# A two-layer hybrid encoder on one core: every TensorE operand moved to a multiple of 512 bytes in SBUF

## The chip, the core and the metric

The kernel runs on one core of one Trainium2 chip. It has five engines that run their own instruction streams and meet at semaphores: TensorE (PE in the profile; PEld is its loading of the stationary operand), VectorE (DVE), ScalarE (ACT), GpSimd (POOL) and SyncE (SP), which issues most of the DMAs. Operands lie in SBUF, a memory of 128 partitions; a tile has an address, which is the byte inside a partition at which it begins. TensorE reads two operands from SBUF for a matmul, the stationary one (128x128 here) and the moving one (128 rows by up to 512 columns), and writes to PSUM. The metric is the device time of one execution in microseconds (us); a time is the median over several runs.

## What is computed

The input is one sequence of 512 positions with 1024 features, in float32. There are two layers, each with a mixer and an MLP, and a last norm:

```python
for layer in range(DEPTH):                      # DEPTH = 2
    h = rms_norm(x, norm_mix[layer])
    y = stick_breaking_attention(h, ...) if layer == 0 else rglru_block(h, ...)
    x = x + y
    h = rms_norm(x, norm_mlp[layer])
    u = relu(h @ w1[layer])                     # 1024 -> 4096
    x = x + (u * u) @ w2[layer]                 # 4096 -> 1024
return rms_norm(x, norm_final)
```

The attention has 16 heads of 64. It takes sigmoids of the scores, a cumulative product of what each key leaves over (from right to left), and sums the values with the weights that result. The second mixer projects to 2048 features, runs a causal convolution with four taps, two gates of block-diagonal 64x64 matrices, and a linear recurrence over the positions (a scan), and multiplies by a gelu branch before its output projection.

## The kernel before

**Precision by halves.** TensorE is fed in a type (float32r) that keeps fewer bits than float32. So each operand is split into a high part (a rounded copy, made by ACT) and a low part (what is left, made by DVE's subtraction), and each product is three matmuls: high by high, low by high and high by low. `three` (L217 to L221) does that for a weight as the stationary operand and 512 positions as the moving one. xgh and xgl hold the halves of the layer's normed input, bh and bl those of the next product's input; these four tiles of 16 KB per partition lie in the pool `const`. Weights come by DMA in slabs of 128 partitions by 1024 numbers (`raw`), and their halves are wh and wl, four of each in the pool `wpool`.

**The MLPs.** Each MLP is cut in four quarters of 1024 hidden features. Most of its products are done by a scheme of seven block products in place of eight (`PRODUCTS`, P1 to P7), whose operands are sums of blocks. In the up products (L966) the weight is stationary and the moving operand has 256 columns: parts of xgh and xgl, or the sums s41 with the low parts `low`, or parts of bh and bl. In the down products (L1061) the hidden features are stationary (bh and bl for the first half, sh and sl for the second) and the weight moves with 512 columns. Helper lines stand for many operations: L757 is the one line in which the class `Ordered` records all of an MLP's DVE and ACT work, so it has to be read by tiles.

**The order.** The order on TensorE is written out by the program. In the attention the products of the next heads are filled in between the scores and values of the current ones by due times (`PACE`, `SCORE0`, `VAL0`); in the second mixer the string `ORDER` gives it; in the MLPs `run` steps through the products and prepares operands up to five products ahead. The other engines' instructions are ordered by a planner, except where the code ties one behind another (`issue_after`, `Ordered`).

**Where tiles lie.** A pool is a stretch of SBUF; pools are laid one behind the other, and a pool that closes gives its place to the next one. Inside a pool the tiles stand in the order in which their tags are first used, `bufs` copies of each, and every tile is rounded up to 32 bytes. The first pool starts at byte 1152. Before the change `const` holds colt (384 bytes), ones and ident (512 each), eps (4), then xgh, xgl, bh, bl, and at its end eight tiles `lams` of 32 bytes. Then follow `wpool` (three raw, four wh, four wl, of 4096 bytes each), `work` (ssq, two sq and two r of 2048 bytes, then the small rt, rc, rp, rn and rr), `home` (eight tiles of 2048 bytes) and the pools of a stage: `hp` and `sp` in the attention, `wmore`, `rp1` and `rp2` in the second mixer, `mlp0` or `mlp1` with `blocks0` or `blocks1` in the MLPs. In `sp` the four `last` tiles (1024 bytes) stand behind three scan tiles of 513 numbers. Ahead of the second MLP's pool a small pool `last` holds three tiles of 4, 48 and 16 bytes.

Of the kernel before, what the change touches and what calls it, by code (L numbers as in the profile page):

```python
# [11 lines left out]
F32 = mybir.dt.float32  # L12
F32R = mybir.dt.float32r
AF = mybir.ActivationFunctionType
ALU = mybir.AluOpType
PSUM = bass.MemoryType.PSUM

P = 128
S = 512
D = 1024  # L20
C = D // P
# [3 lines left out]
EPS = 1e-6  # L25
RG_C = 8.0
SCALE = HD ** -0.5


START = [  # L30
# [31 lines left out]
def hybrid_encoder(  # L62
# [24 lines left out]
    V, A, G, PE = nc.vector, nc.scalar, nc.gpsimd, nc.tensor  # L87

    const = ctx.enter_context(tc.tile_pool(name="const", bufs=1))
    wpool = ctx.enter_context(tc.tile_pool(name="wpool", bufs=4))  # L90
    work = ctx.enter_context(tc.tile_pool(name="work", bufs=2))
# [11 lines left out]
    def f(ap):  # L103
        return ap.bitcast(F32)
# [11 lines left out]
    make_identity(nc, ident)  # L116
    eps_t = const.tile([P, 1], F32, tag="eps", name="eps_t")
    V.memset(eps_t, EPS)

    xgh = const.tile([P, C, S], F32R, tag="xgh", name="xgh")  # L120
    xgl = const.tile([P, C, S], F32R, tag="xgl", name="xgl")
# [19 lines left out]
    class Squares:  # L141
# [21 lines left out]
        def inv_squares(self, ps):  # L163

            for t in range(S // P):
                PE.matmul(
                    ps[:, t : t + 1], self.acc[:, t * P : (t + 1) * P], ones[:, 0:1],
                    start=True, stop=True,
                )
            n = S // P  # L170
            rr = work.tile([P, 2 * n], F32, tag="rr", name="rr", bufs=1)
            V.tensor_scalar(rr[:, :n], ps[:, :n], 1.0 / D, EPS, ALU.mult, ALU.add)
            V.reciprocal(rr[:, :n], rr[:, :n])
            V.tensor_scalar(rr[:, n:], rr[:, :n], -1.0, None, ALU.mult)
            return rr


# [53 lines left out]
    def beside(ws, ah, al, pss, at, ks=range(C)):  # L231
# [8 lines left out]
    ctx.enter_context(tc.manual_schedule(engines={mybir.EngineType.PE}))  # L240


    lams = {
        n: const.tile([P, C], F32, tag=f"lam_{n}", name=n)
        for n in ("ab", "pp", "den", "s1", "s2", "pl", "c8", "c4")
    }
    c8, c4 = lams["c8"], lams["c4"]

    def softplus():

        ab, pp, den, s1, s2, pl, _, _ = lams.values()
        lam = col("lam")

        sigmoid = yield
        V.tensor_scalar(ab, lam, -1.0, None, ALU.mult)
        V.tensor_tensor(ab, ab, lam, ALU.max)
        with tc.issue_after(sigmoid.ins):
            A.activation(pp, ab, AF.Sigmoid, scale=-1.0)
        with tc.issue_after((yield).ins):
            V.tensor_scalar(den, pp, -1.0, 2.0, ALU.mult, ALU.add)  # L260
        V.reciprocal(den, den)
        V.tensor_tensor(s1, pp, den, ALU.mult)
        V.tensor_tensor(s2, s1, s1, ALU.mult)
        V.tensor_scalar(pl, s2, 1.0 / 17, 1.0 / 15, ALU.mult, ALU.add)
        for n in (13, 11, 9, 7, 5, 3, 1):
            V.tensor_tensor(pl, pl, s2, ALU.mult)
            V.tensor_scalar(pl, pl, 1.0 / n, None, ALU.add)
        V.tensor_tensor(pl, pl, s1, ALU.mult)
        V.tensor_scalar(den, lam, -1.0, 0.0, ALU.mult, ALU.max)
        V.scalar_tensor_tensor(c8, pl, 2.0, den, ALU.mult, ALU.add)  # L270
        V.tensor_scalar(c4, c8, RG_C * 0.5, None, ALU.mult)
        V.tensor_scalar(c8, c8, -RG_C, None, ALU.mult)
        yield
# [5 lines left out]
    NB = S // P  # L279
    PAIRS = H // 2  # L280
    half = [slice(0, HD), slice(HD, P)]
    so, early = {}, {}
# [4 lines left out]
    def home_tile(tag, n, name):  # L287
        return home.tile([P, S], F32, tag=tag, name=name, bufs=n)

    with ExitStack() as actx:  # L290
        hp = actx.enter_context(tc.tile_pool(name="hp", bufs=2))
        sp = actx.enter_context(tc.tile_pool(name="sp", bufs=1))


        later = sp.tile([P, S], F32, tag="later", name="later")
        G.memset(later, 0.0)
        G.affine_select(
# [11 lines left out]
        for i in range(2):  # L309
            both = []  # L310
            for nm in ("h", "l"):
                t = sp.tile([P, 2 * P], F32R, tag=f"last{nm}{i}", name=f"last{nm}{i}")
                G.memset(f(t[:, :P]), 0.0)
                both.append(t)
            lasts.append(both)
# [117 lines left out]
        def inverse():  # L433
# [9 lines left out]
            with tc.high_priority():  # L443
                norm["root"] = A.activation(rc, pc[:, :NB], AF.Sqrt, bias=eps_t, scale=1.0 / D)
                V.reciprocal(rc, rc)
                for t in range(NB):
                    ts = slice(t * P, (t + 1) * P)
                    V.tensor_scalar(diag[:, ts], ident, rc[:, t : t + 1], None, ALU.mult)
                V.tensor_scalar(rp, rc, SCALE, None, ALU.mult)
                V.tensor_scalar(rn, rc, -SCALE, None, ALU.mult)  # L450
            norm.update(rc=rc, rp=rp, rn=rn)
# [861 lines left out]
    with ExitStack() as mctx:  # L1313
        mlp = Mlp(mctx, 0)
# [4 lines left out]
        last = {}  # L1319
# [22 lines left out]
        def between(c):  # L1342
            nc.sync.dma_start(out=away[:, c, :], in_=x[c])
            if c == C - 1:
                soft.send(mlp.ready)
# [235 lines left out]


    with ExitStack() as mctx:
        lp = mctx.enter_context(tc.tile_pool(name="last", bufs=1))
        mlp = Mlp(mctx, 1)

        def between(c):

            t = c - 1
            if t not in range(NB):  # L1590
                return
            for h in range(2):
                pt = mlp.bank()
                for i in range(4):
                    PE.transpose(
                        pt[:, i * P : (i + 1) * P], x[4 * h + i][:, t * P : (t + 1) * P], ident
                    )
                A.copy(mlp.y(t, h), pt)
                mlp.begun.add((t // 2 * 2 + h, t % 2))

        gb = []

        def factors():
            for h in range(2):
                gb.append(home_tile(*HOMES[h], "gb"))
                nc.sync.dma_start(
                    out=gb[h], in_=g_final[:, h * S : (h + 1) * S].broadcast_to([P, S])
                )


        A.activation(lp.tile([P, 1], F32, tag="rt", name="early"), eps_t, AF.Sqrt)

        ss = lp.tile([P, NB, 3], F32, tag="ss", name="ss")
        bias = lp.tile([P, NB], F32, tag="bias", name="bias")

        def square(t, h, i, cols=slice(0, S), end=False):

            junk = work.tile([P, S], F32, tag="sq", name="junk")
            A.activation(
                junk[:, cols], mlp.y(t, h)[:, cols], AF.Square, accum_out=ss[:, t, i : i + 1]  # L1620
            )
            if not end:
                A.activation(
                    bias[:, t : t + 1], ss[:, t, i : i + 1], AF.Identity,
                    bias=bias[:, t : t + 1] if i else eps_t, scale=1.0 / D,
                )

        def scaled(t, h, cols=slice(0, S)):
            y = mlp.y(t, h)[:, cols]
            G.tensor_tensor(y, y, gb[h][:, cols], ALU.mult)  # L1630

        def finish(t, h, i, cut=None, last=None):

            ts = slice(t * P, (t + 1) * P)
            rt = work.tile([P, 1], F32, tag="rt", name="rt")
            A.activation(rt, ss[:, t, i : i + 1], AF.Sqrt, bias=bias[:, t : t + 1], scale=1.0 / D)
            V.reciprocal(rt, rt)
            done, y = mlp.y(t, 1 - h), mlp.y(t, h)
            A.activation(done, done, AF.Copy, scale=rt)
            nc.sync.dma_start(out=out[ts, (1 - h) * S : (2 - h) * S], in_=done)  # L1640
            with tc.issue_after(last.ins) if last else nullcontext():
                V.scalar_tensor_tensor(
                    y[:, cut:], y[:, cut:], rt, gb[h][:, cut:],
                    ALU.mult, ALU.mult,
                )
            if cut:
                V.tensor_scalar(y[:, :cut], y[:, :cut], rt, None, ALU.mult)
            nc.sync.dma_start(out=out[ts, h * S : (h + 1) * S], in_=y)

        def end(ws, xs):  # L1650
            for t in range(2):
                square(t, 0, 0)
                scaled(t, 0)
                square(t, 1, 1, end=True)
                finish(t, 1, 1, last=mlp.gained)
            for t in range(2, 4):
                square(t, 1, 0)
                scaled(t, 1)
            for g in range(2):
                mlp.times("P4", g, 0, ws[g], xs[0], False)  # L1660
            mlp.collect("P4", 0, xs[0])
            square(2, 0, 1, end=True)
            finish(2, 0, 1)
            mlp.collect("P4", 1, xs[1])
            for i in range(2):
                cols = slice(i * HS, (i + 1) * HS)
                ps = mlp.bank()[:, :HS]
                for g in range(2):
                    mlp.times("P4", g, 1, ws[g], ps, True, cols)
                mlp.collect("P4", 1, ps, cols)  # L1670
                square(3, 0, 1 + i, cols, end=i == 1)
                if i == 0:
                    scaled(3, 0, cols)
            finish(3, 0, 2, HS)

        end.ready = factors
        mlp.quarters(between, end)
# [69 lines left out]
```

## Time and profile before

| | |
|---|---|
| median of three runs | 1048.85 us (1048.2 to 1051.05) |
| the profiled execution, first to last instruction | span 1047.9 us; its own time is not listed apart from the three runs |
| TensorE busy | 1035.1 us (99%), 5868 matmuls |
| loading of stationary operands | 902.8 us (86%) |
| DVE, ACT, POOL busy | 863.1 us (82%), 701.5 us (67%), 179.2 us (17%) |
| moved by DMA | 159.41 MB, 152 GB/s on average |

Busy times come from one profiled execution. Matmuls overlap: each lasts longer than the distance to the next one's start, because a result needs time to come out of the array. So a matmul's mean duration is not its cost; the distance between the starts of neighbours is, and it is read from the timeline, or from the chain of waits, which merges a run of like matmuls into one row with its length and count ("5.47 PE ps_t L1061 x24"). In a row such as `ps_t<-wh,bh` the names are those of the output, of the moving operand and of the stationary one.

### The profile page before, as it was taken

What the parts mean: (1) busy time and instruction counts of PE and PEld (TensorE: products, weight loads), DVE (VectorE), ACT (ScalarE), POOL (GpSimd) and SP (SyncE); (2) the same over time, 40 slices, a digit from 0 to 9 for tenths busy, and PEclk for the clock granted to TensorE, in tenths of its full rate; (3) what the DMA queues carried; (4) which work ended last, traced back from release to release, by engine and by line L of the source; (5) the groups of instructions that cost most, each with busy time, mean ns of one, the idle gap of its engine ahead of it and who ended that gap; (6) DMA issues with size and microseconds to landing.
All of it is one profiled execution on the core that took longest, in us unless ns stands there. A gap on an engine that the chain in (4) does not pass through costs nothing.

```text
span 1047.9 us, 15859 instructions
## 1 busy us (share of the span) xinstructions
PE 1035.1 (99%) x5868; PEld 902.8 (86%) x5868; DVE 863.1 (82%) x1147; ACT 701.5 (67%) x1082; POOL 179.2 (17%) x238
## 2 busy tenths in 40 slices
PE   8999999999999999999999999999999999999997
PEld 7888888888888988988988788888888988988986
DVE  7888787848788898898899799984789797897897
ACT  6767676836766773773775699964755773773775
POOL 2344344420000010010011121200000010010013
PEclk9999999999999999999999999999999999999999
DMA  6745354537536667567582483352345667567553
GB/s 225 204 137 141 101 149 104 153 109 274 149 80 190 181 139 204 165 140 207 164 208 81 109 214 112 91 221 93 88 86 173 174 142 206 158 139 204 145 125 101
DMA packets 52828, 159.41 MB, mean 152 GB/s; under 512 B 6672, under 2 KB 7952, under 8 KB 52752
## 3 DMA queue, kind: packets, MB, share of 16 engines
q1 hardware_dynamic: 41808, 120.13, 34.4%
q0 software_dynamic: 10368, 37.75, 20.9%
q8 instruction: 46, 0.75, 0.3%
q10 hardware_dynamic: 576, 0.52, 0.2%
q14 instruction: 30, 0.25, 0.1%
HBM read 137.41 MB, written 4.19 MB: 135 GB/s over the span
## 4 chain that ended last, share of the span: by engine, by line
PE 88%; DVE 5%; ACT 3%; issue 2%; DMA 2%; ACTq 0%; POOL 0%; DVEq 0%; POOLq 0%
PE ps_t L1061 14%; PE ps_acc L966 8%; PE ps_z L966 8%; PE ps_acc L1061 7%; PE ps_acc L219 5%; PE ps_acc L221 5%; PE ps_acc L220 5%; PE ps_o L966 5%; PE ps_z L1061 4%; PE ps_o L219 2%; PE ps_t L220 2%; PE ps_o L220 2%; PE ps_o L221 2%; PE ps_t L221 2%; PE ps_t L219 2%
## 5 line engine op out<-in xcount | busy, mean ns | idle before, releaser
L757 ACT CAST wh<-b 128x1024 fp32r<-128x1024 f32 x168 | 174.0, 1047 | 125.6 <-DVE b L757 76.7
L757 DVE TENSOR_TENSOR wl<-b,wh 128x1024 fp32r<-128x1024 f32 x168 | 203.8, 1221 | 50.5 <-ACT wh L757 50.1
L1043 POOL DMA_DIRECT2D b<-in_w_dn x40 | 35.0, 875 | 360.9 <-DVE b L757 204.6
L219 PE MATMUL ps_acc<-xgh,wh 128*128 128x512 f32 x192 | 78.5, 409 | 0.0
L221 PE MATMUL ps_acc<-xgl,wh 128*128 128x512 f32 x192 | 75.2, 392 | 0.0
L220 PE MATMUL ps_acc<-xgh,wl 128*128 128x512 f32 x192 | 75.1, 391 | 0.0
L581 DVE TENSOR_TENSOR_SCAN scan<-keep,later 128x128 f32<-128x128 f32 (+1 forms) x64 | 59.6, 933 | 18.8 <-ACT keep L571 10.9
L214 DVE TENSOR_TENSOR wl<-raw,wh 128x512 fp32r<-128x512 f32 (+2 forms) x70 | 60.9, 895 | 16.2 <-ACT wh L212 16.1
L757 ACT ACTIVATE u<-u 128x512 f32<-128x512 f32 x100 | 63.1, 632 | 6.5 <-DVE u L757 4.8
L212 ACT CAST wh<-raw 128x512 fp32r<-128x512 f32 (+2 forms) x70 | 50.8, 759 | 23.1 <-PE ps_acc L221 7.3
L1043 POOL DMA_DIRECT2D b<-in_w_up x24 | 20.8, 867 | 240.5 <-DVE b L757 72.1
L585 POOL TENSOR_TENSOR w<-w,scan 128x128 f32<-128x128 f32 (+1 forms) x64 | 51.9, 813 | 55.9 <-DVE scan L581 53.2
L757 DVE TENSOR_TENSOR b<-b,b 128x1024 f32<-128x1024 f32 x48 | 58.7, 1224 | 1.3
L757 DVE TENSOR_TENSOR u<-u 128x512 f32<-128x512 f32 (+1 forms) x92 | 54.9, 596 | 2.7 <-ACT u L757 1.1
L966 PE MATMUL ps_z<-xgh,wh 128*128 128x256 f32 x192 | 54.2, 282 | 0.0
L966 PE MATMUL ps_z<-xgh,wl 128*128 128x256 f32 x192 | 54.1, 282 | 0.0
L757 ACT CAST wh<-raw 128x1024 fp32r<-128x1024 f32 x46 | 47.9, 1045 | 9.3 <-PE ps_acc L1061 8.4
L966 PE MATMUL ps_acc<-low,wh 128*128 128x256 f32 x192 | 53.6, 279 | 0.0
L1061 PE MATMUL ps_t<-wl,sh 128*128 128x512 f32 x126 | 50.1, 398 | 0.0
L1061 PE MATMUL ps_t<-wh,sh 128*128 128x512 f32 x126 | 49.6, 394 | 0.0
L1061 PE MATMUL ps_t<-wh,sl 128*128 128x512 f32 x126 | 49.4, 392 | 0.0
L1061 PE MATMUL ps_t<-wh,bh 128*128 128x512 f32 x126 | 49.2, 391 | 0.0
(399 smaller groups left out, 3434.4 us busy)
## 6 DMA issues: line engine op xcount, KB each, us to landing
b<-in_w_dn SPq DMA_DIRECT2D x48, 512.0 KB, 4.5
b<-in_w_dn POOLq DMA_DIRECT2D x40, 512.0 KB, 5.5
b<-in_w_up SPq DMA_DIRECT2D x36, 512.0 KB, 4.6
b<-in_w_up POOLq DMA_DIRECT2D x24, 512.0 KB, 5.3
raw<-in_w_m SPq DMA_DIRECT2D x16, 512.0 KB, 4.1
raw<-in_w_dn SPq DMA_DIRECT2D x16, 512.0 KB, 4.7
raw<-in_w_in SPq DMA_DIRECT2D x16, 512.0 KB, 4.2
raw<-in_w_qk SPq DMA_DIRECT2D x12, 512.0 KB, 3.7
```

Source lines behind the costliest of these rows:

```text
L212: A.copy(wh[:, k, :], raw[:, k, :])
L214: V.tensor_tensor(wl[:, k, :], raw[:, k, :], f(wh[:, k, :]), ALU.subtract)
L219: PE.matmul(ps, wh, ah, start=start, stop=False)
L220: PE.matmul(ps, wl, ah, start=False, stop=False)
L221: PE.matmul(ps, wh, al, start=False, stop=stop)
L581: V.tensor_tensor_scan(sc[:, S - n : S][:, ::-1], keep[:, :n][:, ::-1], later[:, S - n :][:, ::-1], 1.0, ALU.mult, ALU.max,)
L585: G.tensor_tensor(wt, wt, sc[:, S - n + 1 : S + 1], ALU.mult)
L757: ins = getattr(self.e, name)(*args, **kwargs)
L966: PE.matmul(ps[:, i * HS : (i + 1) * HS], m, y, start=new and i == k == n == 0, stop=i == 1 and k == C // 2 - 1 and n == 2, skip_group_che ...
L1043: G.dma_start(out=unit[b].rearrange("p j n -> p (j n)"), in_=unit["src"](to), accum_op=ALU.add)
L1061: PE.matmul(ps, m, y[:, jj, cols], start=first and n == 0, stop=last and n == 2, skip_group_check=not new,)
```

## The change

Small tiles that stood between or behind large ones are gathered ahead of them, and their lengths are chosen so that each pool's large tiles start at a multiple of 512 bytes. ss, bias and the eight lams go to `const`, ahead of xgh; bias is lengthened to 40 numbers. The tile rr is lengthened to 88 numbers, which fills up the small part of `work`. The four `last` tiles go ahead of the scans. The small pool in front of the second MLP is gone; the early square root, which only brings in a table for ACT, writes one element of the tile c0 of that MLP instead of a tile of its own.

```diff
+PAD = 40
+LINE = 88
...
     eps_t = const.tile([P, 1], F32, tag="eps", name="eps_t")
     V.memset(eps_t, EPS)
+    ss = const.tile([P, S // P, 3], F32, tag="ss", name="ss")
+    bias = const.tile([P, PAD], F32, tag="bias", name="bias")
+    lams = {
+        n: const.tile([P, C], F32, tag=f"lam_{n}", name=n)
+        for n in ("ab", "pp", "den", "s1", "s2", "pl", "c8", "c4")
+    }
+    c8, c4 = lams["c8"], lams["c4"]
...
-            rr = work.tile([P, 2 * n], F32, tag="rr", name="rr", bufs=1)
+            rr = work.tile([P, LINE], F32, tag="rr", name="rr", bufs=1)
...
-            V.tensor_scalar(rr[:, n:], rr[:, :n], -1.0, None, ALU.mult)
+            V.tensor_scalar(rr[:, n : 2 * n], rr[:, :n], -1.0, None, ALU.mult)
...
-    lams = {
-        n: const.tile([P, C], F32, tag=f"lam_{n}", name=n)
-        for n in ("ab", "pp", "den", "s1", "s2", "pl", "c8", "c4")
-    }
-    c8, c4 = lams["c8"], lams["c4"]
...
+        last_of = {
+            (nm, i): sp.tile([P, 2 * P], F32R, tag=f"last{nm}{i}", name=f"last{nm}{i}")
+            for i in range(2) for nm in "hl"
+        }
...
-                t = sp.tile([P, 2 * P], F32R, tag=f"last{nm}{i}", name=f"last{nm}{i}")
+                t = last_of[nm, i]
...
-        lp = mctx.enter_context(tc.tile_pool(name="last", bufs=1))
...
-        A.activation(lp.tile([P, 1], F32, tag="rt", name="early"), eps_t, AF.Sqrt)
-
-        ss = lp.tile([P, NB, 3], F32, tag="ss", name="ss")
-        bias = lp.tile([P, NB], F32, tag="bias", name="bias")
+        A.activation(mlp.c[0][:, 0, :1], eps_t, AF.Sqrt)
```

## The prediction

> **What bounds the kernel now.** I read the page first, for the engine that the end hangs on.
>
> ```profile
> span 1047.9 us, 15859 instructions
> PE 1035.1 (99%) x5868; PEld 902.8 (86%) x5868; DVE 863.1 (82%) x1147; ACT 701.5 (67%) x1082; POOL 179.2 (17%) x238
> PE 88%; DVE 5%; ACT 3%; issue 2%; DMA 2%; ACTq 0%; POOL 0%; DVEq 0%; POOLq 0%
> core 0: 1047.9 us, clock 0.996
> ```
>
> TensorE works 99% of the span at a granted clock of 0.996 and makes 88% of the chain that ended last. It does not wait, so only two things can shorten the kernel: fewer matmuls, or a shorter distance from one matmul's start to the next. The change leaves the count alone, so the argument is about that distance. A matmul's mean duration does not give it, because matmuls overlap; the timeline does, as the difference of neighbouring starts.
>
> ```profile
> 399.94 0.39 PE L1061 MATMUL ps_t<-wl,bh 128*128 128x512 f32 x1
> 399.95 0.19 PEld L1061 LDWEIGHTS ps_t<-wh,bl 128*128 128x128 f32 x1
> 400.17 0.39 PE L1061 MATMUL ps_t<-wh,bl 128*128 128x512 f32 x1
> 400.17 0.19 PEld L1061 LDWEIGHTS ps_t<-wh,sh 128*128 128x128 f32 x1
> ```
>
> A 128x512 matmul lasts 0.39 us, but the next starts 0.23 us after it. The load of the next stationary tile starts within 0.01 us of the matmul, so two streams read SBUF together, from two addresses.
>
> Next the chain of waits, which merges runs of matmuls: length divided by count is the distance.
>
> ```profile
> 350.43 2.88 PE ps_acc L966 x24
> 361.75 2.72 PE ps_o L966 x24
> 375.79 2.72 PE ps_acc L1061 x12
> 403.31 2.75 PE ps_z L1061 x12
> 397.84 5.47 PE ps_t L1061 x24
> 832.85 2.82 PE ps_o L966 x24
> 874.82 2.80 PE ps_z L1061 x12
> 869.28 5.55 PE ps_t L1061 x24
> ```
>
> With 256 columns (L966) the distance is 120.0 ns in the first row (moving operand xgh or xgl) and 113.3 in the second (s41 and low). The sixth row is the second row's product in the other MLP: 117.5. With 512 columns (L1061) it is 226.7 in the third row (stationary bh and bl), 229.2 in the fourth (sh and sl) and, for the fourth's counterpart in the other MLP, 233.3. Same code, same shapes, no waiting, and differences of up to 6%.
>
> What differs is the address. Adding up the tiles in the order of the pools (each rounded up to 32 bytes), xgh, xgl, bh and bl start at 32 bytes past a multiple of 512, wpool's wh and wl at 288, and the tiles of the first MLP (s41, sh, sl) at 480, low likewise. In the second MLP the pool of three small tiles opened before it (32+64+32 bytes) pushes s41, sh, sl and one low by 128, to 96. So 2.72 against 2.82, and 2.75 against 2.80, compare one product at two addresses: a shift of 128 bytes cost 4.2 and 4.2 ns per matmul. Addresses above the last 512 bytes change from matmul to matmul inside these runs without changing the distance, so the place within 512 bytes is what counts. The premise of the change holds in this trace.
>
> **The change part by part.** *The gathered tiles.* In the const pool, colt, ones and ident end at a multiple of 512; then eps 32, ss 64, bias 160 and eight lams of 32 are exactly 512, so xgh and all after it start at 0. In the work pool two rt, rc, rp, rn (five times 32) and rr (352) are 512, so home, hp and the rest follow at 0; the last tiles stand ahead of the 2080-byte scans. No instruction is added for this. The rr tile is longer, the operations on it are not.
>
> *The early square root* now writes a corner of c0 instead of a tile of its own.
>
> ```profile
> 693.22 0.62 ACT L151 ACTIVATE ssq<-x 128x512 f32<-128x512 f32 x1
> 693.74 0.19 ACT L1611 ACTIVATE early<-eps_t 128x1 f32<-128x1 f32 x1
> 693.83 0.71 ACT L129 ACTIVATE xgh<-x,colt 128x512 fp32r<-128x512 f32 x1
> ```
>
> It lasts 0.19 us, between the ACT rows of its neighbours. The old tile stood at the same byte that c0 gets, so it waits for the same earlier owner. Later writers of c0 are ACT and DVE operations tens of us on, long after it. I cost it at 0; if the order on ACT shifted, xgh for the next product would come at most 0.2 us later. ss, bias and lams in const have no earlier owner, so waits only go.
>
> *DVE, ACT and the DMAs* get other addresses too. The trace does not show what that does to them. The nearest price is what 128 bytes did to the matmuls, 4.2 of 113.3 ns, 3.7% in either direction; on DVE's 30.0 us in the window shown below that is 28.9 to 31.1, still less than the 32.5 that the window then lasts. I take 0.
>
> *The matmuls* carry the sum. Two rows group most of them: all of L966, then all of L1061 (which has 24 of 256 columns among its 1356).
>
> ```profile
> 0.00:1048.00 1048.00, 239.39 (x2016) 1.00 0.56 152
> 0.00:1048.00 1048.00, 311.19 (x1356) 1.00 0.56 152
> ```
>
> 239.39/2016 = 118.7 ns for 256 columns, 311.19/1356 = 229.5 for 512. From the loops, 2552 of the 5868 matmuls have 256 columns (2016 in L966, 384 for v, 24 at the end of L1061, 128 of scores and values) and 2980 have 512. At the shortest distances that any run shows, 113.3 and 226.7, they would take 2552 x 5.4 = 13.8 us and 2980 x 2.8 = 8.3 us less: 22 us.
>
> Which distance the aligned address gets, no row shows: no fp32r operand lies on a multiple of 512 today. The bounds: one step above (120.0 and 233.3, the longest steady runs) is 2552 x 1.3 + 2980 x 3.8 = 15 us more. Below, the steady distances lie 6.7 ns apart (113.3 and 120.0; 226.7 and 233.3), so one more step would be 106.7 and 220.0: 2552 x 12.0 + 2980 x 9.5 = 59 us less. I take the shortest runs seen. A stream that starts at the edge of a 512-byte stretch touches one stretch fewer than any of today's (1024 bytes from 32, 96, 288 or 480 lie in three, from 0 in two), so it should be no worse than the best of them; that it is better yet is not shown.
>
> *What is late next.* The operands are split by DVE, which has little room in the 256-column stages:
>
> ```profile
> 424.00:458.00 34.00, 34.00 (x261) 32.76 (x261) 30.02 (x32) 28.17 (x39) 4.35 (x5) 1.00 0.61 149
> 816.00:851.00 35.00, 33.97 (x258) 32.54 (x257) 31.01 (x34) 28.27 (x40) 4.33 (x5) 1.00 0.60 144
> ```
>
> (the columns: window, us, PE, PEld, DVE, ACT, POOL). DVE works 30 of 34 us. At 113.3 the first window shrinks to about 32.5, and DVE fits at 92%, with a few late wl. In the second DVE works 31 of 35 and PE already stands 1 us. I take back 2 us of the 22. Forecast: 1047.9 - 22 + 2 = 1028. The median of the three runs, 1048.85, is 0.95 above the profiled span, which I leave for what lies around it: 1029 as a time, 1.9% faster.
>
> *A page against the trace.* The Trainium skill, "SBUF — State Buffer", Specifications, has SBUF in lines of 16 bytes with a price for each new line. Every operand here starts at a multiple of 32 before and after, so by that rule nothing would change: 1049. The rows above disagree (4.2 ns for 128 bytes).
>
> **The rivals.** *One step lower.* If crossing a 512-byte edge costs the step, the aligned streams lose more than the best of today's. For it: the steps are equal for both widths. Against: the last tiles lie at 64 past, on a finer grid than all others, and gain nothing:
>
> ```profile
> 65.55 0.28 PE L629 MATMUL ps_o<-lasth,v 128*128 128x256 f32 x1
> 65.67 0.28 PE L630 MATMUL ps_o<-lastl,v 128*128 128x256 f32 x1
> 65.78 0.34 PE L562 MATMUL ps_z<-kh,q 128*128 128x384 f32 x1
> 85.17 0.28 PE L629 MATMUL ps_o<-th,v 128*128 128x256 f32 x1
> 85.29 0.27 PE L630 MATMUL ps_o<-tl,v 128*128 128x256 f32 x1
> 85.40 0.28 PE L562 MATMUL ps_z<-kh,q 128*128 128x256 f32 x1
> ```
>
> lasth and lastl together take 0.23, as th and tl at 480 do. It would give 59 less, but DVE's 30.0 of 34 would then meet a PE of 30.7, so of the 31 us of the 256-column part I count half: 1049 - 28 - 16 = 1005.
>
> *Slower: the two streams meet.* Aligned, the moving and the stationary operand start at the same place within 512 bytes at the same moment. Where they do so now (th and v, both at 480) the distance is long:
>
> ```profile
> 57.79 0.39 PE L629 MATMUL ps_o<-th,v 128*128 128x512 f32 x1
> 58.02 0.40 PE L630 MATMUL ps_o<-tl,v 128*128 128x512 f32 x1
> 58.26 0.39 PE L562 MATMUL ps_z<-kh,q 128*128 128x512 f32 x1
> ```
>
> 0.47 for two, 235 each. Against it: these are groups of two between other products, and no steady run. If equal places cost every matmul the step, the time is the upper bound, 1049 + 15 = 1064. It decides once the 512-column distance is above 230 with 256 columns not below 118. The Trainium skill, "SBUF — State Buffer", Who interferes with whom, gives PE two independent read ports, which speaks against it; the trace shows a stationary address that changes the distance (226.7, 229.2 and 233.3 with the same moving place, 288), so the trace does not agree that the two streams are apart.
>
> *No difference.* The aligned distance is the mean of today's (229 and 118), or one width gains what the other loses: 1049. The page's rule on lines of 16 bytes, above, ends here too.
>
> **How the numbers follow.** Forecast, about the shortest distances (1018 to 1040): 0.38. One step lower (under 1018): 0.24. No difference: 0.10. Slower: 0.28. The predicted time is the forecast's, 1029. The range leaves out the lowest of the one step lower (DVE losing nothing, below 997) and the part of the slower case that goes beyond its bound: 997 to 1064. Cases of both signs hold most of the chance, so the forecast's own range stands beside it: 1018 to 1040. A difference of 0.3% (3 us) is about what can be told from none. Faster: 0.38 + 0.24 = 0.62; same 0.10; slower 0.28.
>
> **What would show it.** Right: runs of 24 at L966 take 2.72 us in both MLPs, with xgh as with s41, and runs of 12 at L1061 take 2.72, so the two MLPs cost the same. One step lower: 2.56 and 2.64, with PE waiting for wl of DVE at L757. Wrong, and slower: 2.88 and 2.80 or more everywhere, PE still 99% busy. If PE's distances shrink but the span does not, PE's idle time has grown at DVE's wl. Wrong in another way, if DVE's or ACT's means at L757 move with the address.

## The result and the profile after

The changed kernel takes 1049.49 us (median of 12 runs, 1048.5 to 1052.27); the kernel before, run beside it, 1048.75 (12 runs, 1047.42 to 1051.9). The ratio is 1.0006, 95% interval 0.9995 to 1.0016: no difference that can be measured. The forecast was 1029.

The page of the kernel after: span, busy times, the chain by engine, and the granted clock. Every engine's time is within 1.2 us of before, except the weight load's (902.8 then).

```profile
span 1047.0 us, 15859 instructions
PE 1034.0 (99%) x5868; PEld 906.1 (87%) x5868; DVE 862.3 (82%) x1147; ACT 700.4 (67%) x1082; POOL 180.3 (17%) x238
PE 87%; DVE 5%; ACT 3%; issue 2%; DMA 2%; ACTq 0%; POOL 0%; DVEq 0%; POOLq 0%
core 0: 1047.0 us, clock 0.996
```

The page alone would say that the change did nothing. The chain of waits says otherwise. These are the counterparts of the rows shown of before (L966 is now L974, L1061 is L1069; columns: start, length, engine, output, line, count):

```profile
350.05 2.88 PE ps_acc L974 x24
361.57 2.88 PE ps_o L974 x24
375.83 2.72 PE ps_acc L1069 x12
381.27 2.72 PE ps_z L1069 x12
397.59 5.44 PE ps_t L1069 x24
832.91 2.88 PE ps_o L974 x24
869.14 5.44 PE ps_t L1069 x24
874.59 2.72 PE ps_z L1069 x12
```

With 512 columns every run now stands at 226.7 ns, in both MLPs, where before there were 226.7, 229.2 and 233.3. With 256 columns every run stands at 120.0, where s41 and low had 113.3 and 117.5 before. The rows that group a line, L974 and then L1069:

```profile
0.00:1048.00 1048.00, 243.37 (x2016) 1.00 0.57 152
0.00:1048.00 1048.00, 307.46 (x1356) 1.00 0.57 152
```

Against 239.39 and 311.19 before, that is 3.98 us more and 3.73 us less. Added up over the whole trace, from each fp32r matmul's start to the next one's (waits included), the 512-column matmuls went from 696.0 to 691.8 us and those of 256 columns from 304.5 to 308.7. The change moved 4.2 us from one width to the other.

### The profile page after: what moved, and what is told of

Same layout as the page of the kernel before. It is cut to its first block, busy times and chain, and to the rows that moved or that the text cites. A ratio compares the mean times of both kernels' runs of the same rounds, so it can differ in the third digit from the quotient of the medians.

```text
span 1047.0 us, 15859 instructions
## 1 busy us (share of the span) xinstructions
PE 1034.0 (99%) x5868; PEld 906.1 (87%) x5868; DVE 862.3 (82%) x1147; ACT 700.4 (67%) x1082; POOL 180.3 (17%) x238
## 4 chain that ended last, share of the span: by engine, by line
PE 87%; DVE 5%; ACT 3%; issue 2%; DMA 2%; ACTq 0%; POOL 0%; DVEq 0%; POOLq 0%
PE ps_t L1069 14%; PE ps_acc L974 8%; PE ps_z L974 8%; PE ps_acc L1069 7%; PE ps_o L974 5%; PE ps_acc L228 5%; PE ps_acc L230 5%; PE ps_acc L229 5%; PE ps_z L1069 4%; PE ps_t L229 2%; PE ps_o L228 2%; PE ps_t L230 2%; PE ps_t L228 2%; PE ps_o L229 2%; PE ps_o L230 2%
## 5 line engine op out<-in xcount | busy, mean ns | idle before, releaser
L974 PE MATMUL ps_z<-xgh,wh 128*128 128x256 f32 x192 | 54.4, 283 | 0.0
L974 PE MATMUL ps_z<-xgh,wl 128*128 128x256 f32 x192 | 54.4, 283 | 0.0
L974 PE MATMUL ps_acc<-low,wh 128*128 128x256 f32 x192 | 54.4, 283 | 0.0
L1069 PE MATMUL ps_t<-wl,sh 128*128 128x512 f32 x126 | 49.3, 391 | 0.0
L1069 PE MATMUL ps_t<-wh,bh 128*128 128x512 f32 x126 | 49.2, 391 | 0.0
L1069 PE MATMUL ps_t<-wl,bh 128*128 128x512 f32 x126 | 49.1, 390 | 0.0
L1069 PE MATMUL ps_t<-wh,sl 128*128 128x512 f32 x126 | 49.1, 390 | 0.0
```

Source lines behind the costliest of these rows:

```text
L974: PE.matmul(ps[:, i * HS : (i + 1) * HS], m, y, start=new and i == k == n == 0, stop=i == 1 and k == C // 2 - 1 and n == 2, skip_group_che ...
L1069: PE.matmul(ps, m, y[:, jj, cols], start=first and n == 0, stop=last and n == 2, skip_group_check=not new,)
```

## The experiments

### A map of the distances

Three kernels run TensorE alone; each ran once. The first puts the two operands at every pair of multiples of 64 bytes within 512, in runs of 18 matmuls.

> Nothing of the encoder is computed; only TensorE works, in runs of 18 float32r matmuls with the moving and the stationary operand at chosen places within 512 bytes. Theory A (the distance is set by the two places alone): moving 0, stationary 0 gives 120.0 ns at 256 columns and 226.7 at 512, as in the changed kernel; a moving place 192 above the stationary one (480 and 288) gives 113.3 at 256 columns; the distance depends on the difference of the two places. Theory B (the distances come from DVE, ACT and DMA reading SBUF beside TensorE): with these engines idle every pair of places gives one distance per width, near 113.3 and 226.7 or below. Open: whether any pair gives less than 113.3 or 226.7, and whether 64 or 16 bytes are the grain.

Distances in ns, settled part of each run. "Difference" is the stationary operand's place minus the moving one's, modulo 256. The table holds for the 64 pairs of each width (the first two runs, which waited for their operands, left out); pairs of places with the same difference agree within 1.2 ns.

```
difference    0      64            128              192
512 columns   226.7  233.3         232.5            228.9
256 columns   120.0  117.8         118.2 to 119.2   117.8
              (two pairs of odd multiples of 32 at difference 64: 113.3)
```

No pair is below 226.7 or 113.3. At difference 0 the other widths stand at 146.7 (320 columns), 173.4 (384) and 203.0 (448). With N columns, N/2.4 ns and 13.3 more fits these from 256 columns up, except that it gives 200.0 for 448; 128 and 192 columns both stand at 111.7. Only the widths 256 and 512 showed a clear effect of the difference: at differences 0, 64 and 192, 128 and 192 columns kept 111.7, 320 columns 146.7, 384 columns 173.4 to 174.5, and 448 columns 200 to 203.

No DVE or ACT work ran beside these runs, so the other engines do not make the steps, and Theory B falls. Among places that are multiples of 32 it is not the place of one operand that counts, but how far apart the two are. At equal places 512 columns have their shortest distance and 256 columns their longest. On a finer grid the difference is not the whole rule: with both operands at 16, a difference of 0, 512 columns stood at 233.3 and 256 at 118.4. With one operand 4 or 16 bytes away from the other, 512 columns stood at 232 to 237. Theory A had one miss: it expected 113.3 at the difference of 480 and 288, which is 64, and nearly all pairs there stood at 117.8.

The rows of before fit this, with one value left open. Weights lay at 288. xgh and bh at 32 are a multiple of 256 away from them: 120.0 and 226.7. s41 and low at 96 give 192 (117.5). sh and sl as the stationary operand, against weights at 288, give 192 at 480 (229.2) and 64 at 96 (233.3). The open one is s41 and low at 480: they give 64, but had 113.3 and not 117.8. The runs under "What ran before" below deal with that.

### How wide, and how fine

> TensorE alone, as in the first map, in runs of 24. First part: 256 columns, stationary place 0 or 32, moving place in steps of 32, each run behind a run with equal places. Second part: 512 and 256 columns with 128, 96, 64 and 32 columns of the stationary operand, differences 0, 64, 128 and 192 (stationary above moving, modulo 256). Theory A1 (each load of a stationary operand takes a fixed time from the moving stream): the 13.3 ns above N/2.4 stay at 512 columns whatever the stationary's width. Theory A2 (each piece of the stationary operand that is read takes a moment from the moving stream): they shrink with the width, to 10.0, 6.7 and 3.3 ns at 96, 64 and 32 columns, so 223.3, 220.0 and 216.7. For the first part: difference 64 gives 113.3 where both places are odd multiples of 32 and 117.8 where they are multiples of 64, if the grain is 64 bytes; the same everywhere if only the difference counts.

With 256 columns and steps of 32 bytes, differences of 0, 32, 64, 96, 128, 160, 192 and 224 gave 120.0, 118.3, 113.3, 117.2, 119.0, 119.7, 117.8 and 117.8, the same for stationary places 0 and 32. The first kernel had 117.8 at difference 64 for nearly all pairs; here each run stood behind one at difference 0. At the end of the kernel a run at difference 192 stood at 113.3 too. With 512 columns and stationary tiles of 32, 64, 96 and 128 columns the distance at difference 0 was 231.7, 230.0, 230.0 and 226.7: there a narrower stationary tile does not shorten it. At difference 128 it did: 226.7 with 96 columns against 232.9 with 128. With 256 columns, tiles of 32 stood at 113.3 at all four differences. Neither theory (A1, A2) held: the time above N/2.4 does not simply scale with what is loaded, and where it comes from stays open.

### Only the small pool gone

The kernel before, with one of the change's parts: the small pool ahead of the second MLP is dissolved, so that its tiles lie at 480, as in the first.

```diff
+    ss = const.tile([P, S // P, 3], F32, tag="ss", name="ss")
+    bias = const.tile([P, 112], F32, tag="bias", name="bias")
...
-        lp = mctx.enter_context(tc.tile_pool(name="last", bufs=1))
```

> The kernel before with one part of the change alone: the small pool ahead of the second MLP is gone (its two tiles stand at the end of const, which grows by exactly 512 bytes), so in the second MLP s41, sh, sl and low lie at 480 past a multiple of 512 as in the first, and all else at its old place within 512. Theory A (places alone set the distances): the second MLP's 24 matmuls of s41 and low take 2.72 us in place of 2.82, its 12 of sh and sl 2.75 in place of 2.80; over 288 matmuls at 4.2 ns and 342 at 4.2 ns that is 2.6 us off: about 1046, ratio 0.9975. Theory B (the address has nothing to do with it, the second MLP is slower for another reason): the rows stay at 2.82 and 2.80, ratio 1.000.

1047.17 us against 1048.86, ratio 0.9982 (0.9970 to 0.9994). The chain of waits, second MLP: s41 and low, then bh and sh in turn.

```profile
906.31 2.74 PE ps_o L968 x24
911.88 2.72 PE ps_o L968 x24
925.91 2.72 PE ps_acc L1063 x12
928.63 2.75 PE ps_t L1063 x12
```

The same rows of the kernel before:

```profile
905.99 2.83 PE ps_o L966 x24
911.65 2.82 PE ps_o L966 x24
925.80 2.72 PE ps_acc L1061 x12
928.52 2.80 PE ps_t L1061 x12
```

The rows took the forecast values (2.72 and 2.75), so Theory B falls. This part alone saves 1.7 us by its medians, where 2.6 were expected; the whole change shows nothing of that.

### All at one place, but not on 512

The changed kernel, everything from xgh on 64 bytes higher.

```diff
+    const.tile([P, 16], F32, tag="gap", name="gap")
     xgh = const.tile([P, C, S], F32R, tag="xgh", name="xgh")
```

> The changed kernel with one gap of 64 bytes ahead of xgh, so that every operand lies at 64 past a multiple of 512 and none on it; all differences of places stay 0. Theory of the difference: nothing changes against the changed kernel: 120.0 ns for 256 columns, 226.7 for 512, 1049.5 us. The reason that the prediction gave (a stream that starts at the edge of 512 bytes touches one stretch fewer): a stream of 2048 bytes from 64 touches five stretches where the one from 0 touches four, so the 512-column distance would rise from 226.7 by up to one step, to 229 to 233, and the time to 1056 to 1068.

1049.94 us against 1049.07, ratio 1.0004 (0.9992 to 1.0016). Its rows for the two lines:

```profile
0.00:1052.00 1052.00, 243.36 (x2016) 1.00 0.56 152
0.00:1052.00 1052.00, 307.45 (x1356) 1.00 0.56 152
```

They are those of the changed kernel to 0.01 us. So the multiple of 512 by itself does nothing.

### The hidden features level with the weights, nothing else

The kernel of "only the small pool gone" with a gap of 64 bytes ahead of sh and sl, which brings them to difference 0. No operand lies on a multiple of 512.

```diff
+                    self.bp.tile([P, 16], F32, tag="gap", name="gap", bufs=1)
```

> The kernel before with the small pool gone, as in the run before this, and a gap of 64 bytes ahead of sh and sl, so that these lie at 32 (256 away from the moving weights at 288); nothing is at a multiple of 512. Theory A: L1061 goes to 226.7 ns in both MLPs, the runs of s41 and low stay at 113.3; 684 matmuls of sh and sl by 2.2 to 2.5 ns are 1.6 us off the run before this one: about 1045.5, ratio to the kernel before 0.9967. Theory D (it is the multiple of 512 that gives 226.7): L1061 stays at 229, ratio 0.998.

1047.14 us, ratio 0.9983 (0.9972 to 0.9993). The down line fell from 309.77 us in the kernel without the gap to 308.51, the up line stayed at 238.52 in both. So the multiple of 512 is not what gives 226.7, and Theory D falls. The 1.6 us that Theory A expected of the time did not show: the times of the two kernels cannot be told apart. The row of sh that was 2.75 above:

```profile
927.24 2.72 PE ps_t L1064 x12
```

### The weights alone moved

The changed kernel with a gap of 64 bytes at the end of const and rr shortened by as much: only wpool moves, so most differences become 64 (weight stationary) or 192 (weight moving).

```diff
-LINE = 88
+LINE = 72
...
+    const.tile([P, 16], F32, tag="gap", name="gap")
```

> The changed kernel with all of wpool 64 bytes higher and all else at multiples of 512. Theory A: where the weight is stationary (about 1390 matmuls of 512 columns at L228 to L230) the difference is 64 and the distance 233.3 in place of 226.7; where it moves (1332 at L1069) the difference is 192 and the distance 228.9; the 2016 of 256 columns at L974 go from 120.0 to 117.8 and the 384 of v to 117.8. Sum 9.2 + 2.9 - 4.4 - 0.8 = 7 us more: 1056, ratio to the kernel before 1.0065; if the 256-column ones go to 113.3, 13.4 in place of 4.4, 2 us less: 1047. Theory C (the span does not follow the distances): 1.000.

1053.17 us, ratio 1.0042 (1.0026 to 1.0058). All of 512 columns together took 701.2 us (9.4 more than the changed kernel), all of 256 columns 303.7 (5.0 less). The net is 4.4 us more, between the two sums of the expectation (7 more and 2 less). Up products (L975) and down products (L1070), each from two stages:

```profile
362.48 2.83 PE ps_o L975 x24
888.29 10.92 PE ps_acc L975 x96
376.59 2.80 PE ps_acc L1070 x12
454.92 2.75 PE ps_acc L1070 x12
```

Each width has two distances at one difference of places. Of the 1452 up matmuls in unbroken runs of one kind, about 580 stood at 113.3 to 114 and the others at 117.8; the second row, at 113.8 each, is of the first sort. With 512 columns the down products stood at 228.9 as in the map, except between 374 and 390 us and between 849 and 885 us, where they stood at 233.3 (third row). The rows do not show why. The loss with 512 columns and the gain with 256 show that the two widths move in opposite directions in the kernel too.

### Each width at its better difference

The changed kernel with home and the pools of the stages 192 bytes past a multiple of 512 (s41 and low at difference 64) and sh and sl back at difference 0 by a gap.

```diff
-LINE = 88
+LINE = 136
...
+                    self.bp.tile([P, 16], F32, tag="gap", name="gap", bufs=1)
```

> The changed kernel with one part undone: the moving operands s41 and low (and the rest of home and the stage pools) lie 192 past a multiple of 512, so the stationary operand is 64 above them modulo 256 as it was before; sh and sl are kept at a multiple of 256 by a gap of 64 bytes. Theory A (difference modulo 256 alone): L1069 keeps 226.7 ns, the s41 and low runs of L974 go from 120.0 to 117.8 as in the map, or to 113.3 as in the kernel before; over 576 matmuls of s41 and low and as many mixed ones at half the price that is 1.9 to 5.8 us off the changed kernel: 1047.5 to 1043.7, ratio to the kernel before 0.995 to 0.9985. Theory C (the span is held by something other than the distances, so that their gains never arrive): 1.000.

1045.85 us (12 runs, 1045.02 to 1049.01) against 1048.96, ratio 0.9972 (0.9961 to 0.9982): 0.3% below the kernel before, run beside it, and inside the range of Theory A. In its chain of waits one stage has both short distances:

```profile
352.73 2.88 PE ps_z L975 x24
355.61 2.74 PE ps_o L975 x24
361.17 2.72 PE ps_o L975 x24
375.20 2.72 PE ps_acc L1070 x12
377.93 2.72 PE ps_t L1070 x12
```

xgh (first row) is at difference 0 still, 120.0. That suggested the next step.

### The input of the MLPs moved too

On top of that, the MLPs see xgh and xgl through a view 192 bytes past a multiple of 256, the mixers through one at 0.

```diff
+    room_h = const.tile([P, C * S + 48], F32R, tag="xgh", name="xgh")
+    room_l = const.tile([P, C * S + 16], F32R, tag="xgl", name="xgl")
+    at = lambda t, n: t[:, n : n + C * S].rearrange("p (c s) -> p c s", c=C)
+    xgh, xgl = at(room_h, 0), at(room_l, 16)
+    mxh, mxl = at(room_h, 48), at(room_l, 0)
...
-                return xgh[:, c, ts], xgl[:, c, ts]
+                return mxh[:, c, ts], mxl[:, c, ts]
```

> Built on e2a_sums_at_192. In the MLPs the halves of the normed input (xgh, xgl) are written and read through a view that lies 192 past a multiple of 256, in the mixers through the view at 0, as before; a gap of 64 bytes puts the gates of the second mixer level with their inputs. Theory of the difference (stationary place minus moving place, modulo 256): the 1056 matmuls of 256 columns with xgh or xgl in the MLPs go from 120.0 to between 113.3 and 117.8 ns, 2.3 to 7.1 us less; the 384 of 512 columns in the first quarters of the MLPs go from 226.7 to 233.3, 2.5 us more; the gates and their neighbours 0.6 us less. From e2a's 1045.85 this gives 1041 to 1045.5; I take 1042.5. Rival: DVE, which works 30 of 34 us in the 256-column stages, becomes the bound there; then the distances fall in the undisturbed runs, PE stands for weights, and the time stays at 1045 to 1047.

1050.34 us, ratio 1.0009 (0.9997 to 1.0021). Both theories missed: by its median it is 4.5 us slower than the kernel it was built on. The rows of the same products:

```profile
354.26 2.83 PE ps_acc L979 x24
357.08 2.83 PE ps_z L979 x24
359.91 2.83 PE ps_o L979 x24
365.56 2.83 PE ps_o L979 x24
```

Nearly all up runs stand at 117.8; only in the first up stage of the second MLP (806 to 850 us) about 150 matmuls stood near 113.3. xgh gained 2.2 ns where I had hoped for up to 6.7, and s41 and low, untouched in their difference of 64, lost 4.5. The two nearly cancel: between 345 and 560 us the 256-column matmuls average 117.6 ns in the kernel it was built on and 117.8 here. Nothing waits inside these runs.

The 384 matmuls of 512 columns in the first quarters of the MLPs rose to about 233 as expected, 2.5 of the 5.1 us by which that width's total grew between the two traces. Most of the rest lies in the first 40 us, where the 512-column matmuls took 29.7 us against 26.7. The granted clock between 20 and 40 us was 0.83 in this trace and 1.00 in the other, so that part does not come from the places. What makes up the rest of the 4.5 us between the medians was not settled. One difference of places has two distances; the next run asks whether what runs before decides.

### What ran before

> TensorE alone; nothing of the encoder is computed, the output is one of its sums. Runs of 72 matmuls of 256 columns at a difference of 64, each behind 12 matmuls of 512 columns and then a short run that differs: of 512 columns at differences 0, 64 and 192; of 24 with 256 columns at differences 0, 128 and 192; of 1, 3, 6 and 12 with 256 columns at difference 0; of 24 with 128 columns and of 12 with 384 columns at difference 0; and at the end one of 400, and four pairs of 24 in which difference 0 and difference 64 take turns. Theory of two steady states (what ran just before decides): behind 24 of 256 columns at difference 0 the 72 stand at 113.3 ns, behind 512 columns at 117.8, and each holds to the end of its run; behind 12 it is 113.3 still, behind 1 it is open. Rival (the distance follows from the places alone, and the 117.8 of e4_x_moved came from VectorE and ScalarE beside it): all runs settle at one value, 113.3.

In equal windows the number of matmuls that start tells the two distances apart (7 us hold 59.4 at 117.8 and 61.8 at 113.3; the counts in brackets include those still under way at the edges). The windows of TensorE lie inside the runs of 72 behind: 512 columns at difference 192; 24 of 256 columns at difference 0; one such; three such; the last row is the run of 400.

```profile
66.50:73.50 7.00, 7.00 (x62) 7.00 (x61) 0.00 (x0) 0.00 (x0) 1.00 0.00 0
80.80:87.80 7.00, 7.00 (x64) 7.00 (x63) 0.00 (x0) 0.00 (x0) 1.00 0.01 2
119.40:126.40 7.00, 7.00 (x62) 7.00 (x61) 0.00 (x0) 0.00 (x0) 1.00 0.00 0
131.00:138.00 7.00, 7.00 (x64) 7.00 (x63) 0.00 (x0) 0.00 (x0) 1.00 0.01 2
215.00:257.00 42.00, 42.00 (x373) 42.00 (x372) 0.00 (x0) 0.00 (x0) 1.00 0.00 1
```

Starts in the trace give 117.8 for the first and third, 113.3 for the others, each to the end of its run, 400 matmuls included. Three matmuls at difference 0 were enough for the short state, one was not. 512 columns at difference 64, 384 and 128 columns at difference 0 and 256 columns at difference 128 also led into it; 512 and 256 columns at difference 192 led into the long one. I had expected the long state behind 512 columns of any difference, and that was too wide. The rival (the places alone decide) falls.

This accounts for s41 and low in the kernel before, which had 113.3 at a difference of 64: they ran between products of xgh at difference 0. It does not account for the 113.3 and the 233.3 in parts of "The weights alone moved".

### The short state set on purpose

The kernel of the moved input, with the order inside the product P6 changed: its 16 matmuls with bh, which are at difference 0, run first, then its 8 with low.

```diff
-                        PE.matmul(
-                            ps[:, i * HS : (i + 1) * HS], m, y,
...
+                        parts.append((n // 2 if block == 3 else 0, i, m, y))
+            parts.sort(key=lambda part: part[0])
```

> Built on e4_x_moved. One thing more: in the product P6 (moving operand bh, at a difference of 0, with low at 64) the 16 matmuls with bh come first and the 8 with low after them, where they took turns two to one. Theory of two steady states: those 16 bring TensorE into the shorter state, as 3 and more did in m3_history, and the runs behind them at a difference of 64, 11 of 14 in each of six stages, go from 117.8 to 113.3 ns: 6 x 11 x 24 x 4.5 ns = 7.1 us less than e4_x_moved's 1050.34, 1043.2. Rivals: the state does not hold beside working VectorE and ScalarE, and the time stays at 1050; or VectorE, 30 of 34 us busy in these stages, cannot follow, TensorE waits for weights, and the time comes to 1046 to 1048 with the runs of 24 at 2.72 us.

1048.64 us, ratio 0.9998 (0.9989 to 1.0007). Windows of one stage, up line alone, of the kernel of the moved input and then of this one:

```profile
346.00:361.00 15.00, 15.00 (x130) 1.00 0.68 180
```

```profile
342.00:357.00 15.00, 15.00 (x134) 1.00 0.69 193
```

The state was set: starts lie 113.3 apart behind P6 in all six stages, beside working DVE and ACT, so the first rival falls. All 256-column matmuls together went from 306.5 to 301.8 us. But the time fell by 1.7 us and not by 7.1. The chain by engine, and waits of the weight load (columns: who, for whom, us in total, times, longest):

```profile
PE 65%; DVE 16%; ACT 11%; issue 4%; DMA 3%; ACTq 0%; SPq 0%; POOL 0%; DVEq 0%; POOLq 0%
...
PEld ps_t L1076 <- DVE wl L769: 3.6, 6, 0.7
PEld ps_acc L1076 <- DVE wl L769: 2.4, 7, 0.4
PEld ps_z L1076 <- DVE wl L769: 2.3, 8, 0.4
```

```profile
PEld ps_t L1074 <- DVE wl L769: 2.0, 5, 0.4
PEld ps_z L1074 <- DVE wl L769: 0.8, 2, 0.4
```

The second fence is the kernel before this step: 2.8 us in 7 waits at the down line became 8.3 in 21. On the matmuls themselves that cost 3.8 us: from start to start, those of 512 columns at the down line took 308.0 us in place of 304.2. TensorE's share of the chain is 65%, DVE's 16% (87% and 5% there). The shorter up stages leave DVE late with wl for the down products. The theory had the state right and the second rival had the wait right; neither had the time.

### All kernels in one view

Sums of the distances of all fp32r matmuls of a width, span of the same execution, and median time, in us:

```
                                  512 col  256 col  span    median
before                            696.0    304.5    1047.9  1048.75
after                             691.8    308.7    1047.0  1049.49
only the small pool gone          695.4    304.4    1046.8  1047.17
... and hidden features level     694.1    304.0    1045.3  1047.14
weights alone moved               701.2    303.7    1051.4  1053.17
all at one place, not on 512      691.7    308.0    1047.1  1049.94
each width at its better          691.4    305.1    1043.7  1045.85
input of the MLPs moved too       696.5    306.5    1050.8  1050.34
short state set on purpose        698.4    301.8    1046.9  1048.64
```

The span minus the two sums is between 46.5 and 47.8 in all nine. That alone proves little, because the sums run from start to start and hold the waits; it says that the 336 other matmuls and the two ends took the same everywhere. Sums and spans are also of one execution each, and the granted clock differs between them: between 20 and 40 us it was 0.83 in "input of the MLPs moved too", 1.00 in "each width at its better" and "short state set on purpose", and 0.91 in the others. So a microsecond or two between two rows need not come from the places. That distances make the time rests on the medians of the kernels in which only tiles moved. With the weights alone moved, the sums are 4.4 us above those of before and the median 4.2 above that of the kernel before, run beside it; with each width at its better, 4.0 and 3.1 below.

## Why the prediction was wrong

**What held.** The bound: TensorE at 99% before and after, and the chain still runs through its matmuls. The 512-column half of the step "The matmuls carry the sum": all aligned runs at the down line have 226.7, as forecast. The early square root at 0: it lasts the same 0.19 us and stands at the same place between its neighbours on ACT, and no wait came of it.

```profile
693.04 0.61 ACT L160 ACTIVATE ssq<-x 128x512 f32<-128x512 f32 x1
693.56 0.19 ACT L1618 ACTIVATE c<-eps_t 128x1 f32<-128x1 f32 x1
693.65 0.71 ACT L138 ACTIVATE xgh<-x,colt 128x512 fp32r<-128x512 f32 x1
```

DVE, ACT and the DMAs at 0: DVE and ACT were busy for 862.3 and 700.4 us against 863.1 and 701.5, and the DMAs moved 152 GB/s in both.

**The step that failed** is the choice inside "The matmuls carry the sum": "I take the shortest runs seen", for 256 columns. The aligned distance is 120.0, the longest of the steady runs, not 113.3. In place of 13.8 us less, the 256-column matmuls cost 4.2 more. The reason given for the choice ("a stream that starts at the edge of a 512-byte stretch touches one stretch fewer") does not hold: with everything at 64 past a multiple of 512 the two lines take the same 243.36 and 307.45 us. Nor does the premise ahead of it, that "the place within 512 bytes is what counts". The rows compared there were two products whose tiles had moved by 128 bytes against weights that had not; they could not tell a place from a difference of places. That the distance took three values (226.7, 229.2, 233.3) with the moving place at 288 throughout was even written down, as an argument that the streams meet; a difference of places fits it.

**A term that was mis-sized.** 8.3 us for 512 columns used L1061's mean for all 2980. But xgh and bh lay at 32 and their weights at 288, a multiple of 256 apart: those products were at 226.7 already, as the third of the rows of before shows for bh. Only sh and sl, small groups, and runs of bh in the second MLP had something to gain. Those of bh stand behind sh at 233.3 there and begin with some six matmuls between 228 and 236 before they settle at 226.7, so twelve of them average 229.0. The measured gain is 4.2, of which 3.73 in L1061.

**The 2 us of DVE.** Not called upon here, since the 256-column stages grew longer. Where they were made shorter, in the last experiment, the late wl came as described: 5.5 us more of waits of the weight load at the down line, 3.8 us on its matmuls.

**The rivals.** "No difference", in its second form (one width gains what the other loses), is what happened, and it had 0.10; that the two amounts come out nearly equal is chance, a matter of how many matmuls of each kind this kernel has. "Slower: the two streams meet" had the right variable, equal places, and the right value for 256 columns (120.0, 2.88 for 24). Its price for 512 columns went wrong: it came from the pairs of th and v (235), which the prediction itself said were no steady run. They were the first matmuls behind others: in the run of TensorE alone, 512 columns at difference 0 behind another group mostly begin with 230 to 236 for three to five matmuls and then stand at 227. "One step lower" did not happen; no pair of the map shows less than 113.3 and 226.7. The rule that the prediction cited from the Trainium skill, "SBUF — State Buffer", Specifications (lines of 16 bytes), gave the right time for another reason: by it nothing would move, and the rows moved in both directions.

## What to carry to other kernels

When a matmul's distance seems to depend on an address, compare the two operands' addresses with each other before either with a grid, and look for two rows in which only one of them moved. Aligning everything sets every difference to zero, which here is the best value for 512 columns and, of differences in steps of 64, the worst for 256; placing the tiles by who meets whom, width by width, gave 0.3% where alignment gave none. And a gain worked out from the shortest steady runs counts only for the matmuls that do not have that distance already, so count those.

## What was not expected of the hardware

- With fp32r operands, a new stationary tile for each matmul and places that are multiples of 32, the distance depends on the difference of the two places modulo 256: 226.7, 233.3, 232.5 and 228.9 ns for 512 columns at 0, 64, 128 and 192. With both places at 16 it was 233.3, so equal places alone are not enough. With 320 columns it was 146.7 at differences 0, 64 and 192 alike.
- At difference 0 the distance fits N/2.4 ns and 13.3 more for 256, 320, 384 and 512 columns (120.0, 146.7, 173.4, 226.7). The Trainium skill, "TensorE: Matmul & The Clock Gate", Back-to-back issue gap, gives N/2.4 and about 2.5 ns for an isolated gap, and about 131 ns for pairs of load and matmul at 512 columns; no steady run here is as short.
- With 256 columns at difference 64 there are two steady states, 113.3 and 117.8 ns, and the one that is entered held for 400 matmuls. Three matmuls of 256 columns at difference 0 led into the shorter one. With 512 columns at difference 192 the kernel with the weights moved showed two values as well, 228.9 and 233.3. What makes the states was not found.
